# Retention of each head spread over 31 chunks of one row of main products; q, k, v and gate tiles claimed at their eviction

## The chip, the cores and the metric

The kernel runs on one core of a Trainium2 chip. The metric is device time in microseconds (us) of one execution. Three runs of the kernel before took 2264.44, 2265.14 and 2267.26 us; the median is 2265.14 us. One further execution, taken with the profiler, has a span of 2264.8 us and a time of 2266.59 us.

## The reference, cut to what matters

One layer of a decoder trunk for 256 prompt rows and 8 sample rows, so that every activation has 264 columns. The part that the change touches is the retention mixer of eight heads:

```python
h = _rmsnorm(x, norm1_g) * (1.0 + scale1) + shift1
q, k, v, gr, u, ga, gb = split(h @ w_in)
q, k = rotary(q), rotary(k) * RET_QK_DIM ** -0.5
scores = einsum('bhld,bhmd->bhlm', q, k) * decay
o = einsum('bhlm,bhmv->bhlv', scores, v) + einsum('bhld,bhdv->bhlv', q_dec, S)
S_new = gamma ** L * S + einsum('bhmd,bhmv->bhdv', k_dec, v)
y_a = (group_norm_heads(o, gn_g) * silu(gr)) @ w_proj_a
mixed = sigmoid(ga) * y_a + sigmoid(gb) * y_b
x = x + gate1 * (mixed @ w_out)
```

A head has 256 q and k columns and 512 v and gate columns. The states of the eight sample rows are read, updated and written head by head.

## The kernel before

**Products.** Every large product is made of chunks. A chunk loads 512 KB of weights (`w_...`, four blocks of 128 rows by 256 columns), splits them into a rounded part `wh_...` on ACT (line 216) and a rest `wl_...` on DVE (line 217), three buffers of each, and then issues 24 matmuls of 128x264 (line 198). A matmul triple is `wh` times the rounded activation, `wh` times its rest, and `wl` times the rounded activation, so the second matmul of a chunk already needs both parts of the activation. All these matmuls go through `mm`, which ties each to the one before it: on PE they stand in program order. Work that does not go through `mm`, as the matmuls and transposes of the retention, is placed by the scheduling layer wherever it judges it ready. The layer fixes the order of each engine's instructions when the program is built.

**The head stage.** It makes q, k, v and gate of heads 1 to 7 (`head_group`, six groups of four chunks: q, k, two of v, two of gate; head 0's come from the stage before), then the eight groups `gate_a`. Row `h` of the loop holds the groups of head h+1, and from row 1 the eight chunks `project(h-1, g)` of the previous head's output with `w_proj_a` (accumulators `acc_pa`): four after the k group, four after the first v group. Row 0 has 24 chunks, rows 1 to 6 have 32, row 7 has 32 and eight more of `gate_a`.

**Retention.** `retention(h, mods)` returns 19 steps, which `spread` deals out evenly behind the chunks of row h. The first steps are `sample_rows` (transposes `vsp`), `scores` (`scp`, then `sclo`/`schi` on DVE and ACT) and the transposes `vtp`, `ktp` of v and k with their splits `vh`, `vl`, `kh`, `kl`. Then come eight `sample(b)` (512 KB of state in and out on POOL's queue, `S` and `vb` on DVE and ACT), `prompt_out` (matmuls `op`) and `prompt_state` (`sp`), `sample_q` (`qp`) and `sample_out` (`osp`).

The last two steps are `centre` and `gate`, the group norm:

```python
mu = head_sum(o, "mu")                      # s_mu, split into s_hi_mu, s_lo_mu; two matmuls mean_mu on PE
ve.scalar_tensor_tensor(out=o, in0=mu...)   # o minus the mean, line 709
sc.activation(out=st["t4"], in_=o, func=AF.Square)
var = head_sum(st["t4"], "var")             # s_var, s_hi_var, s_lo_var; two matmuls mean_var
sc.activation(out=r, in_=var, func=AF.Sqrt, ...)
ve.reciprocal(out=r, in_=r)
ve.tensor_tensor(out=gr, in0=gr, in1=r...)  # line 724
split_act(gr, yh, yl)                       # yh on ACT, line 228; yl on DVE, line 229
```

`yh` and `yl` are what `project(h, g)` multiplies.

**Tiles.** q, k, v and gate tiles come from a pool of two buffers each. Before, the four tiles of head h+1 are claimed together at the start of row h.

Of the kernel before, what the change touches and what calls it, by code (L numbers as in the profile page):

```python
# [20 lines left out]
F32 = mybir.dt.float32  # L21
# [4 lines left out]
P = 128  # L26

D = 2048
KT = D // P
TP = 256  # L30
NS = 8
T = TP + NS
H = 8
# [11 lines left out]
G_Q, G_K, G_V, G_GR, G_U, G_GA, G_GB = 0, 8, 16, 32, 48, 56, 64  # L45
# [44 lines left out]
def spread(main, side, by=1.0):  # L90

    out, done = [], 0
    for i, step in enumerate(main):
        out.append(step)
        upto = min(int(len(side) * (i + 1) / (by * len(main))), len(side))
        out += side[done:upto]
        done = upto
    return out + side[done:]


def run(steps):
    for step in steps:
        step()


def call(f, *args):
    return lambda: f(*args)
# [22 lines left out]
def build(ctx, tc, a):  # L130
# [78 lines left out]
    def split_chunk(src, name, nk=4):  # L209
        w = raw_chunk(src, f"w_{name}", nk)  # L210
        return split_loaded(w, name, nk)
# [19 lines left out]
    def gemm_part(acc, hi, lo, xh, xl, k0, nk, first, last):  # L231

        for b in range(2):
            for k in range(nk):
                cols = slice(b * P, (b + 1) * P)
                s, e = first and k == 0, last and k == nk - 1
                mm(out=acc[:, b, :T], lhsT=hi[:, k, cols], rhs=xh[:, k0 + k, :], start=s, stop=False)
                mm(out=acc[:, b, :T], lhsT=hi[:, k, cols], rhs=xl[:, k0 + k, :], start=False, stop=False)
                mm(out=acc[:, b, :T], lhsT=lo[:, k, cols], rhs=xh[:, k0 + k, :], start=False, stop=e)

    def new_acc(name):
        n_acc[0] += 1
        return acc_ring[n_acc[0] % len(acc_ring)].tile([P, 2, 512], F32, tag="acc", name=f"acc_{name}")

    def gemm(src, gs, xh, xl, nk, name, use, apart=False):

        accs = {}
        nch = nk // 4

        def chunk(g, c):  # L250
            if c == 0:
                accs[g] = Halves([new_acc(f"{name}_{g}_{b}") for b in range(2)]) if apart else new_acc(f"{name}_{g}")
            hi, lo = split_chunk(src[g, c], f"{name}_{g}_{c}")
            gemm_part(accs[g], hi, lo, xh, xl, 4 * c, 4, c == 0, c == nch - 1)
            if c == nch - 1:
                use(g, accs[g])

        return [call(chunk, g, c) for c in range(nch) for g in gs]
# [81 lines left out]
    def rstd_from(pn, name):  # L340

        r = keep.tile([P, T], F32, tag="rstd", name=f"rstd_{name}")
        mark[name] = sc.activation(out=r, in_=pn[:, :T], func=AF.Sqrt, bias=eps[:, 0:1], scale=1.0 / D)

        for t in (slice(TP, T), slice(0, TP)) if name == "n2" else (slice(0, T),):
            ve.reciprocal(out=r[:, t], in_=r[:, t])
        return r
# [26 lines left out]
    h_hi = acts.tile([P, KT, T], F32R, tag="a_hi", name="h_hi")  # L374
    h_lo = acts.tile([P, KT, T], F32R, tag="a_lo", name="h_lo")
# [6 lines left out]
    hq = hd.enter_context(tc.tile_pool(name="qkvg", bufs=2))  # L382
    raw_q, raw_k, raw_v, raw_gr = {}, {}, {}, {}

    def head_tiles(h):
        raw_q[h] = hq.tile([P, 2, T], F32, tag="q", name=f"q{h}")
        raw_k[h] = hq.tile([P, 2, T], F32, tag="k", name=f"k{h}")
        raw_v[h] = hq.tile([P, 4, T], F32, tag="v", name=f"v{h}")
        raw_gr[h] = hq.tile([P, 4, T], F32, tag="gr", name=f"gr{h}")

    def head_groups(h):
        return [
            (G_Q + h, raw_q[h][:, 0:2]), (G_K + h, raw_k[h][:, 0:2]),
            (G_V + 2 * h, raw_v[h][:, 0:2]), (G_V + 2 * h + 1, raw_v[h][:, 2:4]),
            (G_GR + 2 * h, raw_gr[h][:, 0:2]), (G_GR + 2 * h + 1, raw_gr[h][:, 2:4]),
        ]


    with tc.tile_pool(name="pooling", bufs=1) as pl:
# [9 lines left out]
        for i in range(4):  # L409
            k = slice(4 * i, 4 * i + 4)  # L410
# [10 lines left out]
        for j in range(2):  # L421
            mark["pn"] = te.matmul(out=pn[:, :T], lhsT=ones, rhs=sgb[:, j, :], start=j == 0, stop=j == 1)
        r1 = rstd_from(pn, "n1")
        head_tiles(0)
        groups = [(G_U + g, ue[g // 2][:, 2 * (g % 2):2 * (g % 2) + 2, 15:]) for g in range(8)]
        groups += head_groups(0)
        groups += [(G_GB + g, sgb[:, 2 * g:2 * g + 2, :]) for g in range(8)]

        def start_mods(k0, nk):
# [124 lines left out]
    def rotate(x0, x1, dst, scale, name):  # L554
        cos, sin = rot[:, 0:T], rot[:, T:2 * T]
        tt = hp.tile([P, 4, T], F32, tag="t4", name=f"rot_{name}")
        for i, (s, t) in enumerate(((x0, cos), (x1, sin), (x1, cos), (x0, sin))):
            ve.scalar_tensor_tensor(out=tt[:, i, :], in0=s, scalar=scale, in1=t, op0=ALU.mult, op1=ALU.mult)
        ve.tensor_tensor(out=dst[:, 0, :], in0=tt[:, 0, :], in1=tt[:, 1, :], op=ALU.subtract)
        ve.tensor_tensor(out=dst[:, 1, :], in0=tt[:, 2, :], in1=tt[:, 3, :], op=ALU.add)  # L560

    def head_use(h, n, src):

        dst = head_groups(h)[n][1]
        if n < 2:
            rotate(src[:, 0, :], src[:, 1, :], dst, (1.0, DQK ** -0.5)[n], f"{n}_{h}")
        elif n >= 4:
            sc.activation(out=dst, in_=src, func=AF.Silu)
        elif h:
            sc.copy(out=dst, in_=src)  # L570

    def head_group(h, n):
        return gemm(a["w_in"], [head_groups(h)[n][0]], h_hi, h_lo, KT, "in",
                    lambda g, acc: head_use(h, n, acc[:, :, :T]))

    y = {}
# [173 lines left out]
    def gate_a(g):  # L750
        def use(_, acc):
            s = hp.tile([P, 2, DV], F32, tag="S", name=f"sga{g}", bufs=4)[:, :, :T]
            sc.activation(out=s, in_=acc[:, :, :T], func=AF.Sigmoid)
            sy.dma_start(out=dram["sga"][:, 2 * g:2 * g + 2, :], in_=s)

        return gemm(a["w_in"], [G_GA + g], h_hi, h_lo, KT, "ga", use)

    later = [s for i in (SC2, SH2) for s in mod2_steps(i)[1]]
    for n in range(6):
        head_use(0, n, head_groups(0)[n][1])  # L760
    for h in range(H):
        if h + 1 < H:
            head_tiles(h + 1)
            groups = [head_group(h + 1, n) for n in range(6)]
        else:
            groups = [gate_a(g) for g in range(8)]
        proj = [call(project, h - 1, g) for g in range(8)] if h else []
        mods = later[2 * h:2 * h + 2]
        main = groups[0] + groups[1] + proj[0:4] + groups[2] + proj[4:8] + groups[3] + groups[4] + groups[5]
        run(spread(main, retention(h, mods)))  # L770
        for g in groups[6:]:
            run(g)


    m_hi = acts.tile([P, KT, T], F32R, tag="a_hi", name="m_hi")
# [1 line left out]
    for g in range(8):  # L777
        k = slice(2 * g, 2 * g + 2)
# [98 lines left out]
    with tc.tile_pool(name="ffn", bufs=1) as fp:  # L877
# [19 lines left out]
        def conv_gate(i, u, cso, scv):  # L897

            c = fp.tile([P, 2, T], F32, tag="t2", name=f"cv{i}", bufs=4)
            for b in range(2):  # L900
                f = i + b * FB
                sc.activation(out=c[:, b, :], in_=u[:, b, :T], func=AF.Identity, scale=cw[:, 2, b, i:i + 1],
                              bias=vec[:, V_CB + f:V_CB + f + 1])
                for j in (1, 2):
                    ve.scalar_tensor_tensor(out=c[:, b, j:TP], in0=u[:, b, 0:TP - j], scalar=cw[:, 2 - j, b, i:i + 1],
                                            in1=c[:, b, j:TP], op0=ALU.mult, op1=ALU.add)
            ve.tensor_copy(out=cso[:, :, i % FG, 0:10], in_=u[:, :, TP - 2:T])
            ve.tensor_tensor(out=c[:, :, TP:T], in0=c[:, :, TP:T], in1=scv[:, :, i % FG, :], op=ALU.add)
            s = fp.tile([P, T], F32, tag="t1", name=f"ffs{i}", bufs=2)
            sc.activation(out=s, in_=c[:, 0, :], func=AF.Silu)  # L910
            ve.tensor_tensor(out=s, in0=s, in1=c[:, 1, :], op=ALU.mult)
            split_act(s, f_hi[:, i, :], f_lo[:, i, :])
            if i % FG == FG - 1:
                gp.dma_start(out=a["conv_out"][:, i // FG], in_=cso)

        rest = [call(gt2, 9, 1), call(gt2, 10), call(gt2, 12), call(gt2, 14)]
        for i0 in range(0, FB, FG):
            state = conv_state(i0 // FG)
            pairs = [[i0, i0 + 1]] if i0 == 0 else [[i0], [i0 + 1]]
            main = [s for gs in pairs + [[i0 + 2], [i0 + 3]]  # L920
                    for s in gemm(a["w_up"], gs, h2_hi, h2_lo, KT, "up", lambda g, acc: conv_gate(g, acc, *state))]
# [40 lines left out]
        for g in range(8):  # L962
            k = slice(2 * g, 2 * g + 2)
# [94 lines left out]
```

## Time and profile before

| | |
|---|---|
| median of 3 runs | 2265.14 us |
| profiled execution: time, span | 2266.59 us, 2264.8 us |
| PE (TensorE matmul) busy | 2236.0 us, 99% |
| PEld (TensorE weight load) busy | 2141.7 us, 95% |
| DVE (VectorE) busy | 1506.8 us, 67% |
| ACT (ScalarE) busy | 1094.3 us, 48% |
| POOL (GpSimd) busy | 222.7 us, 10% |
| head stage | about 460 to 1340 us |

A matmul's own duration is longer than the distance to the next one, since matmuls overlap; a chunk's duration is read from the chain of waits, which counts each matmul up to the start of the next. Each clock level has a share: granted clock 1.00 is 2.4 GHz, 0.50 is 1.2 GHz.

### The profile page before, as it was taken

How to read it: one execution, taken by the hardware profiler on the slowest of the kernel's cores; microseconds unless marked ns; L12 is line 12 of the kernel's file. 1: busy time of each engine (PE TensorE's matmuls, PEld its weight loads, DVE VectorE, ACT ScalarE, POOL GpSimd, SP SyncE). 2: the span in 40 equal slices, each digit the busy share in tenths (PEclk: the TensorE clock that was granted, in tenths of full speed). 3: DMA queues.
4: the chain of work that ended last, by engine and by line, in shares of the span. 5: the costliest groups of instructions: out<-in, count | busy, mean ns of one | idle time of the engine just before them, and what ended most of it. 6: DMA issues, size and time to landing. Idle time of an engine off the chain costs nothing.

```text
span 2264.8 us, 44898 instructions
## 1 busy us (share of the span) xinstructions
PE 2236.0 (99%) x18432; PEld 2141.7 (95%) x18432; DVE 1506.8 (67%) x2170; ACT 1094.3 (48%) x1380; POOL 222.7 (10%) x386
## 2 busy tenths in 40 slices
PE   8999999999999999999999999999999999999998
PEld 6899999898999999999999999899999999999998
DVE  6666775685768686868777767676666666654444
ACT  4333454354655555555556554455444444443343
POOL 0000222011101010101010101110000100000000
PEclk9999999999999999999999999999999999999999
DMA  9777867798787887878787879755656666565562
GB/s 337 245 269 260 280 195 266 283 352 311 253 297 255 290 272 270 297 258 311 249 300 252 304 264 350 261 191 183 199 186 216 209 189 211 183 191 193 184 193 100
DMA packets 168254, 561.14 MB, mean 248 GB/s; under 512 B 18448, under 2 KB 28752, under 8 KB 168048
## 3 DMA queue, kind: packets, MB, share of 16 engines
q1 hardware_dynamic: 144048, 474.08, 62.1%
q0 software_dynamic: 23568, 83.73, 10.4%
q8 instruction: 144, 2.36, 0.4%
q10 hardware_dynamic: 432, 0.46, 0.1%
q14 instruction: 62, 0.51, 0.1%
HBM read 509.82 MB, written 48.38 MB: 246 GB/s over the span
## 4 chain that ended last, share of the span: by engine, by line
PE 74%; DVE 1%; DMA 1%; issue 0%; ACT 0%; SPq 0%; DVEq 0%; ACTq 0%
PE acc_up L198 23%; PE acc_in L198 18%; PE acc_dn L198 11%; PE acc_pa L198 7%; PE acc_wo L198 4%; PE acc_ga L198 4%; PE mp L198 2%; DMA w_in<-in_w_in 1%; PE acc_dn L954 1%; PE qp L198 0%; PE scp L600 0%; DVE wl_in L217 0%; PE op L641 0%; PE op L642 0%; PE sp L651 0%
## 5 line engine op out<-in xcount | busy, mean ns | idle before, releaser
L198 PE MATMUL acc_up<-h_hi,wh_up 128*128 128x264 f32 x1408 | 400.3, 284 | 0.0
L198 PE MATMUL acc_up<-h_lo,wh_up 128*128 128x264 f32 x1408 | 399.3, 284 | 0.0
L198 PE MATMUL acc_up<-h_hi,wl_up 128*128 128x264 f32 x1408 | 399.0, 283 | 0.0
L198 PE MATMUL acc_in<-h_hi,wh_in 128*128 128x264 f32 x1344 | 385.8, 287 | 1.1 <-ACT wh_in L216 1.1
L198 PE MATMUL acc_in<-h_hi,wl_in 128*128 128x264 f32 x1344 | 382.7, 285 | 3.9 <-DVE wl_in L217 3.9
L198 PE MATMUL acc_in<-h_lo,wh_in 128*128 128x264 f32 x1344 | 383.6, 285 | 0.0
L217 DVE TENSOR_TENSOR wl_up<-w_up,wh_up 128x1024 fp32r<-128x1024 f32 x176 | 216.0, 1227 | 181.3 <-ACT wh_up L216 181.2
L216 ACT CAST wh_up<-w_up 128x1024 fp32r<-128x1024 f32 x176 | 184.6, 1049 | 251.6 <-issue 149.7
L217 DVE TENSOR_TENSOR wl_in<-w_in,wh_in 128x1024 fp32r<-128x1024 f32 x168 | 204.5, 1219 | 128.5 <-ACT wh_in L216 127.5
L216 ACT CAST wh_in<-w_in 128x1024 fp32r<-128x1024 f32 x168 | 176.0, 1049 | 193.4 <-DMA w_in<-in_w_in 92.5
L198 PEld LDWEIGHTS acc_up<-h_hi,wh_up 128*128 128x128 f32 x1408 | 264.8, 188 | 4.2 <-issue 2.5
L198 PEld LDWEIGHTS acc_up<-h_lo,wh_up 128*128 128x128 f32 x1408 | 265.0, 188 | 0.0
L198 PEld LDWEIGHTS acc_up<-h_hi,wl_up 128*128 128x128 f32 x1408 | 264.4, 188 | 0.0
L198 PEld LDWEIGHTS acc_in<-h_hi,wh_in 128*128 128x128 f32 x1344 | 254.3, 189 | 8.9 <-ACT wh_in L216 5.4
L198 PEld LDWEIGHTS acc_in<-h_hi,wl_in 128*128 128x128 f32 x1344 | 253.8, 189 | 4.9 <-DVE wl_in L217 4.8
L198 PEld LDWEIGHTS acc_in<-h_lo,wh_in 128*128 128x128 f32 x1344 | 254.3, 189 | 0.2
L198 PE MATMUL acc_st<-h_hi,wh_st 128*128 128x264 f32 x704 | 202.1, 288 | 1.0 <-ACT h_hi L363 1.0
L198 PE MATMUL acc_st<-h_hi,wl_st 128*128 128x264 f32 x704 | 200.3, 286 | 1.3 <-DVE wl_st L217 1.3
L198 PE MATMUL acc_st<-h_lo,wh_st 128*128 128x264 f32 x704 | 200.2, 285 | 0.0
L198 PE MATMUL acc_dn<-f_lo,wh_dn 128*128 128x264 f32 x680 | 192.9, 284 | 0.0
L198 PE MATMUL acc_dn<-f_hi,wl_dn 128*128 128x264 f32 x680 | 192.8, 284 | 0.0
L198 PE MATMUL acc_dn<-f_hi,wh_dn 128*128 128x264 f32 x680 | 192.8, 284 | 0.0
(273 smaller groups left out, 5357.8 us busy)
## 6 DMA issues: line engine op xcount, KB each, us to landing
wm<-in_w_mod SPq DMA_DIRECT2D x176, 512.0 KB, 6.3
w_up<-in_w_up SPq DMA_DIRECT2D x176, 512.0 KB, 4.2
w_in<-in_w_in SPq DMA_DIRECT2D x168, 512.0 KB, 5.9
w_dn<-in_w_down SPq DMA_DIRECT2D x88, 512.0 KB, 3.6
S<-in_state_ret POOLq DMA_DIRECT2D x64, 512.0 KB, 5.7
out_rs<-S POOLq DMA_DIRECT2D x64, 512.0 KB, 6.4
w_pa<-in_w_proj_a SPq DMA_DIRECT2D x64, 512.0 KB, 4.2
w_st<-in_w_in SPq DMA_DIRECT2D x66, 384.0 KB, 4.2
```

The lines of the kernel that those rows point to most:

```text
L198: ins = te.matmul(**kw)
L216: c = sc.copy(out=hi, in_=w)
L217: t = ve.tensor_tensor(out=lo, in0=w, in1=hi.bitcast(F32), op=ALU.subtract)
L954: te.matmul(out=accs[b][:, 0, t], lhsT=w[:, k, cols], rhs=f[:, kk, t], start=False, stop=e and not n, skip_group_check=n > 0)
```

## The change

The rows of the loop become one list `main` of 256 chunks, in the same order as before. Head h's retention is dealt out behind chunks 31h to 31h+30 of this list, whatever row they belong to, and the last eight chunks have no retention beside them. Head 0's 19 steps thus lie behind 31 chunks in place of 24, those of each other head behind 31 in place of 32. Where row h+1 begins at chunk 24+32h, head h's last step `gate` stands behind chunk 31h+30, and the first `project(h, 0)` is chunk 32h+32. Before, `gate` stood behind chunk 32h+23. The tiles of head h+1 are claimed one by one, each just before its first writing.

```diff
-    def head_tiles(h):
-        raw_q[h] = hq.tile([P, 2, T], F32, tag="q", name=f"q{h}")
...
+    def head_tile(h, n):
+
+        if n == 0:
+            raw_q[h] = hq.tile([P, 2, T], F32, tag="q", name=f"q{h}")
+        elif n == 1:
+            raw_k[h] = hq.tile([P, 2, T], F32, tag="k", name=f"k{h}")
+        elif n == 2:
+            raw_v[h] = hq.tile([P, 4, T], F32, tag="v", name=f"v{h}")
+        elif n == 4:
+            raw_gr[h] = hq.tile([P, 4, T], F32, tag="gr", name=f"gr{h}")
...
     def head_use(h, n, src):
 
-        dst = head_groups(h)[n][1]
+        if h:
+            head_tile(h, n)
+        dst = head_part(h, n)
...
+    main = []
     for h in range(H):
-        if h + 1 < H:
-            head_tiles(h + 1)
-            groups = [head_group(h + 1, n) for n in range(6)]
-        else:
-            groups = [gate_a(g) for g in range(8)]
+        groups = [head_group(h + 1, n) for n in range(6)] if h + 1 < H else [gate_a(g) for g in range(8)]
         proj = [call(project, h - 1, g) for g in range(8)] if h else []
-        mods = later[2 * h:2 * h + 2]
-        main = groups[0] + groups[1] + proj[0:4] + groups[2] + proj[4:8] + groups[3] + groups[4] + groups[5]
-        run(spread(main, retention(h, mods)))
-        for g in groups[6:]:
-            run(g)
+        main += groups[0] + groups[1] + proj[0:4] + groups[2] + proj[4:8] + sum(groups[3:], [])
+
+    share, steps, done = 31, [], 0
+    for i, chunk in enumerate(main):
+        chunk()
+        h = i // share
+        if i % share == 0 and h < H:
+            steps, done = retention(h, later[2 * h:2 * h + 2]), 0
+        upto = len(steps) * (i % share + 1) // share if h < H else len(steps)
+        run(steps[done:upto])
+        done = upto
```

Lines after the diff's first part move by 6 to 12; `mean_var` is line 702 before and 711 now, `op` 640 to 642 and 649 to 651.

On PE, the end of head 0's group norm and the start of its projection stand like this before. The fence has the second `mean_var` and what follows it, then the end of the stretch; between the two stand 141 matmuls of `acc_in` in all, with `vsp`, `scp`, `vtp` and `ktp` of head 1 among them.

```order
L702 MATMUL mean_var_6438<-s_lo_var_6435,ones_r 128x264
L198 MATMUL acc_in_6457<-h_hi,wh_in_2_6529 128x264
L198 MATMUL acc_in_6457<-h_lo,wh_in_2_6529 128x264
...
L198 MATMUL acc_in_6606<-h_hi,wl_in_3_6741 128x264
L198 MATMUL acc_pa_0_6775<-yh_6449,wh_pa_0_6778 128x264
L198 MATMUL acc_pa_0_6775<-yl_6450,wh_pa_0_6778 128x264
```

The same place on PE now, without a gap:

```order
L198 MATMUL acc_in_6547<-h_hi,wl_in_3_6676 128x264
L711 MATMUL mean_var_6658<-s_hi_var_6654,ones_r 128x264
L711 MATMUL mean_var_6658<-s_lo_var_6655,ones_r 128x264
L598 MATMUL vsp_6745<-cst,vsc_6743 128x128 x4
L609 MATMUL scp_6818<-q_5569,k_5751 128x256 x2
L609 MATMUL scp_6818<-q_5569,k_5751 128x128 x2
L619 MATMUL vtp_0_6860<-cst,v_5919 128x128 x4
L619 MATMUL vtp_1_6869<-cst,v_5919 128x128 x4
L198 MATMUL acc_pa_0_6711<-yh_6669,wh_pa_0_6714 128x264
L198 MATMUL acc_pa_0_6711<-yl_6670,wh_pa_0_6714 128x264
```

Of the 141 chunk matmuls between `mean_var` and the first `acc_pa` none is left; only head 1's `vsp`, `scp` and `vtp` stand there.

On DVE, head 0's group norm from its mean to `yl` reads like this now (`rot_2_6704` and `k_6703` are the rotation of the k group whose product `acc_in_6547` ends just ahead of `mean_var` on PE):

```order
L718 SCALAR_TENSOR_TENSOR o_5830<-mean_mu_6615,o_5830 128x1056
L217 TENSOR_TENSOR wl_pa_1_6756<-w_pa_1_6753,wh_pa_1_6755 128x1024
L730 SCALAR_TENSOR_TENSOR gr_158<-gr_158,vec,o_5830 128x264 x4
L704 TENSOR_TENSOR s_var_6651<-t_0_6619 128x528
L217 TENSOR_TENSOR wl_pa_2_6788<-w_pa_2_6785,wh_pa_2_6787 128x1024
L705 TENSOR_TENSOR s_var_6651<-s_var_6651 128x264
L565 SCALAR_TENSOR_TENSOR rot_2_6704<-acc_in_6547,rot 128x264 x4
L229 TENSOR_TENSOR s_lo_var_6655<-s_var_6651,s_hi_var_6654 128x264
L566 TENSOR_TENSOR k_6703<-rot_2_6704 128x264
L567 TENSOR_TENSOR k_6703<-rot_2_6704 128x264
L728 RECIPROCAL gnr_6661<-gnr_6661 128x264
L733 TENSOR_TENSOR gr_158<-gr_158,gnr_6661 128x1056
```

The next row there is `yl`. Before, the same stretch was:

```order
L695 TENSOR_TENSOR s_var_6431<-t_0_6398 128x528
L217 TENSOR_TENSOR wl_in_1_6491<-w_in_1_6488,wh_in_1_6490 128x1024
L696 TENSOR_TENSOR s_var_6431<-s_var_6431 128x264
L217 TENSOR_TENSOR wl_in_2_6530<-w_in_2_6527,wh_in_2_6529 128x1024
L229 TENSOR_TENSOR s_lo_var_6435<-s_var_6431,s_hi_var_6434 128x264
L217 TENSOR_TENSOR wl_in_3_6560<-w_in_3_6557,wh_in_3_6559 128x1024
L217 TENSOR_TENSOR wl_in_0_6610<-w_in_0_6607,wh_in_0_6609 128x1024
L719 RECIPROCAL gnr_6441<-gnr_6441 128x264
```

Before, the splits between `s_var` and the reciprocal are those of v chunks that PE multiplies meanwhile; now they are splits of the projection's own weights, and the rotation of k has moved ahead of `s_lo_var`.

On DVE at the end of head 4's group norm, from the reciprocal to `yl`, the order is now:

```order
L728 RECIPROCAL gnr_11618<-gnr_11618 128x264
L672 STREAM_SHUFFLE vb_0_11915<-vsr_11706 128x512
L611 TENSOR_TENSOR dec_11768<-scp_11770,dec_11768 128x384
L733 TENSOR_TENSOR gr_10063<-gr_10063,gnr_11618 128x1056
L565 SCALAR_TENSOR_TENSOR rot_6_11811<-acc_in_11668,rot 128x264 x4
L675 SCALAR_TENSOR_TENSOR S_0_11913<-vb_0_11915,k_10528,S_0_11913 128x512 x2
L217 TENSOR_TENSOR wl_pa_2_11927<-w_pa_2_11924,wh_pa_2_11926 128x1024
L229 TENSOR_TENSOR vl_0_11824<-vtp_0_11818,vh_0_11823 128x512
L229 TENSOR_TENSOR sclo_11777<-dec_11768,schi_11776 128x384
L229 TENSOR_TENSOR vl_1_11833<-vtp_1_11827,vh_1_11832 128x512
...
L229 TENSOR_TENSOR yl_11627<-gr_10063,yh_11626 128x1056
```

Three small rows (`k`, `kl_0`, `k`) stand where the line of dots is; `vb_0`, `S_0`, `dec`, `vl` and `sclo` belong to head 5's retention, which has moved into this stretch.

The number of chunk matmuls that PE has between the second `mean_var` of head h and its first `acc_pa` is now 0, 0, 0, 13, 23, 47, 78 and 102 for heads 0 to 7; after the first `acc_pa` matmul of heads 2, 4 and 5 stand 24 matmuls `op` of the next head's `prompt_out`, in head 3 two, ahead of the second.

## Rows read from the trace of the kernel before

**Rows 1.** The page's head and part 1: busy us, share of the span, instructions.

```profile
span 2264.8 us, 44898 instructions
PE 2236.0 (99%) x18432; PEld 2141.7 (95%) x18432; DVE 1506.8 (67%) x2170; ACT 1094.3 (48%) x1380; POOL 222.7 (10%) x386
```

**Rows 2.** Waits of PE, 420 to 640 us: total us, times, longest.

```profile
PE acc_in L198 <- DVE wl_in L217: 3.9, 4, 2.2
```

**Rows 3.** Stretches: us; busy us (instructions) by engine; granted clock; DMA share; GB/s.

```profile
467.55:470.95 3.40, 3.40 (x18) 3.40 (x18) 0.60 (x4) 1.69 (x2) 3.33 (x6) 0.50 0.99 371
543.40:556.30 12.90, 9.74 (x78) 8.44 (x69) 8.17 (x11) 6.92 (x8) 0.00 (x0) 1.00 0.76 274
556.30:559.70 3.40, 3.40 (x18) 3.40 (x17) 3.30 (x7) 1.10 (x2) 0.00 (x0) 0.50 0.77 286
```

**Rows 4.** Chain of waits, 525 to 760 us: start, us, what.

```profile
549.16 2.91 PE acc_in L198 x24
...
591.41 0.11 PE op L642
...
664.82 0.12 PE mean_mu L702
...
675.75 0.12 PE mean_var L702
...
677.84 0.44 PE vsp L589 x4
...
679.98 1.31 PE scp L600 x8
...
687.11 0.87 PE vtp L610 x8
...
694.04 2.43 PE acc_pa L198 x20
```

**Rows 5.** DVE in order of time, 664 to 700 us: start, us, instruction, idle before.

```profile
665.25 1.25 DVE L709 SCALAR_TENSOR_TENSOR o<-mean_mu,o 128x1056 f32<-128x1056 f32 x1
...
667.55 1.70 DVE L721 SCALAR_TENSOR_TENSOR gr<-gr,vec,o 128x264 f32<-128x264 f32 x4
669.16 0.70 DVE L695 TENSOR_TENSOR s_var<-t 128x528 f32<-128x528 f32 x1
...
670.92 0.43 DVE L696 TENSOR_TENSOR s_var<-s_var 128x264 f32<-128x264 f32 x1
...
672.71 0.43 DVE L229 TENSOR_TENSOR s_lo_var<-s_var,s_hi_var 128x264 fp32r<-128x264 f32 x1
...
676.42 1.80 DVE L719 RECIPROCAL gnr<-gnr 128x264 f32<-128x264 f32 x1 [0.71 <-ACT gnr L718]
678.14 1.16 DVE L217 TENSOR_TENSOR wl_in<-w_in,wh_in 128x1024 fp32r<-128x1024 f32 x1
679.22 1.24 DVE L724 TENSOR_TENSOR gr<-gr,gnr 128x1056 f32<-128x1056 f32 x1
680.38 1.44 DVE L558 SCALAR_TENSOR_TENSOR rot<-acc_in,rot 128x264 f32<-128x264 f32 x4
...
684.65 1.25 DVE L229 TENSOR_TENSOR yl<-gr,yh 128x1056 fp32r<-128x1056 f32 x1
685.82 1.41 DVE L666 SCALAR_TENSOR_TENSOR S<-vb,k,S 128x512 f32<-128x512 f32 x2
...
690.53 1.27 DVE L229 TENSOR_TENSOR vl<-vtp,vh 128x512 fp32r<-128x512 f32 x2
```

**Rows 6.** ACT in order of time, 664 to 700 us: start, us, instruction, idle before.

```profile
666.53 1.09 ACT L712 ACTIVATE t<-o 128x1056 f32<-128x1056 f32 x1 [1.05 <-DVE o L709]
...
674.47 1.28 ACT L718 ACT_TABLE_LOAD   x1
675.90 0.48 ACT L718 ACTIVATE gnr<-mean_var,eps 128x264 f32<-128x264 f32 x1 [0.15 <-PE mean_var L702]
...
681.81 1.05 ACT L228 CAST yh<-gr 128x1056 fp32r<-128x1056 f32 x1
```

## What I predict, and how

> **What bounds the kernel now.** I read the page first. PE is busy in 99% of the span and no other engine above 67%, its own weight loads apart [rows 1], so the time is PE's stream of matmuls, and a change can only shorten it by closing gaps in that stream, or lengthen it by opening some. Then I read PE's waits in the head stage: from 420 to 640 us there are four for a split on DVE, 3.9 us in all, the longest 2.2 us [rows 2]. Stretches show what such a gap costs. From 543.4 to 556.3 us, the end of head 0's retention, PE is busy 9.74 us of 12.9, so 3.2 us are open; right behind it, from 556.3 to 559.7, the granted clock is 0.50 with 18 matmuls in 3.4 us. The same fall stands at 467.55 us, before any retention runs [rows 3]. At full clock a chunk of 24 takes 2.91 us, 0.121 us each [rows 4], so 3.4 us hold 28; the second fall costs 10 to 12 matmuls, 1.2 to 1.5 us. I use 1.4.
>
> Head 0 is thus the one place with something to win: 3.2 + 1.4 = 4.6 us.
>
> **What the change does, part by part.** The number of matmuls, splits, state transfers and bytes is unchanged. Claiming a tile at its eviction adds no instruction. It could only matter where an eviction waits for the old buffer's reader, and retention h has left q, k, v and gate of head h some chunks before head h+2 writes them; I count it as nothing, and if that cover were gone it would be one chunk, 2.9 us, of waiting per head at most.
>
> *The gain.* Head 0's 19 steps get 31 chunks in place of 24. Its states and splits are less dense and the 4.6 us can go. I take the whole of it; the bounds are 0 and 4.6.
>
> *The loss.* Project(h) is not moved, but the gate that makes its input is moved to a later place, by 7 chunks for head 0 and one chunk less for every later head. What PE has between the second mean_var and the first acc_pa is what hides the end of the group norm. Before, it is 141 matmuls for head 0 (17 us) and 126 for the others: in head 1, mean_var ends at 675.87 us and acc_pa starts at 694.04, 18.2 us later, while yl is ready at 684.65 + 1.25 = 685.90 [rows 4, 5]. That is 10.0 us of work behind 18.2 us of cover. Now the cover is 0, 0, 0, 13, 23, 47, 78 and 102 matmuls, and what follows in PE's order is acc_pa.
>
> The Trainium skill, page "PSUM — Partial Sum Buffer", section "Engine vs sequencer instructions", says that matmuls start and complete in program order and that ScalarE and VectorE take their queues strictly first in, first out. By this rule no later chunk can fill the gap; without it, the gaps below would vanish. The open 3.2 us at 543.4, where PE waits with other chunks queued behind, agree.
>
> *Head 0.* I start at the end of mean_mu and add up DVE's new order. Successive rows start 0.08 us before the end of the one ahead (678.14 + 1.16 against 679.22) [rows 5], so a row counts its time less 0.08: o 1.17, a split 1.08, gr 1.62, s_var 0.62, a split 1.08, s_var 0.35, the rotation of k 1.36, s_lo 0.43, in all 7.7 us until the second mean_var. ACT's square of 1.09 us lies beside gr [rows 6]. PE has 27 matmuls left there, 3.3 us, and one mean_var of 0.1: open 4.3. From that mean_var on: 0.15 to the root on ACT, root 0.48, reciprocal 1.72, product 1.24, yh 1.05, yl 1.25, with four handovers of about 0.03: 6.0 us. The table load of 1.28 us is done while ACT waits [rows 6]. PE has mean_var 0.1, vsp 0.44, scp 1.31, vtp 0.87 and one acc_pa, together 2.9 [rows 4]: open 3.1. Head 0 loses 7.4 us.
>
> *Head 1.* The same with 41 matmuls (5.0 us) behind mean_mu and one more split ahead of s_lo: 8.8 + 6.0 − 5.0 − 0.1 − 2.9 = 6.8 us.
>
> *Heads 2 to 5.* There mean_var is in time (in head 2, 78 matmuls or 9.4 us of cover against about 9). Behind it DVE's list is again mixed with splits, rotation and the next head's first steps, so I take the 10.0 us measured in head 1 of before. Cover in PE: vsp, scp, vtp 2.6, ktp about 0.2 and one acc_pa 0.1; in heads 2, 4 and 5 the 24 op of 0.11 (2.7 us) [rows 4]; and the matmuls counted above. Head 2: 10.0 − 5.6 = 4.4. Head 3: 13 matmuls are 1.6 us, two op 0.2, so 10.0 − 4.7 = 5.3. Head 4: 23 matmuls are 2.8 us and the cover 8.4, but its list from the reciprocal to yl holds S (1.41), vl (1.27), sclo and kl (about 0.5 each) and one split fewer than in head 1: 2.3 us more, and on ACT a state of about one microsecond and the table load of 1.28 stand ahead of the root. I take 13.4 − 8.4 = 5.0. Head 5: 47 matmuls, 11.3 us of cover against 10 to 13: 1.0. Heads 6 and 7 have over 12 us of cover: nothing.
>
> The open times sum to 7.4 + 6.8 + 4.4 + 5.3 + 5.0 + 1.0 = 29.9 us.
>
> *The clock.* A gap of 3.2 us, in two parts, is followed by one fall of the clock [rows 3]. Heads 0 to 4 each have a gap at least as long, so I add one fall each, 5 × 1.4 = 7.0. The bounds are none, since a fall inside a wait costs nothing, and two falls each, 14.
>
> *Sum.* 29.9 + 7.0 − 4.6 = 32.3 us on the profiled execution's 2266.6: 2298.9. The median of the runs is 1.45 us below that execution; the forecast is 2297.5 us, slower.
>
> **Rivals.**
>
> *A, faster: the head stage only gets smoother.* The relief of head 0 decides alone, and gate is ready when acc_pa comes: 2265.1 − 4.6 = 2260.5 us. For it speaks that every gap of PE in this stage lies in head 0. It needs at most 4.6 us of new gaps, so a chain from mean_mu to yl of some 8 us in heads 0 and 1 where the rows give 13.7. Against it stand those rows. Chance 5%.
>
> *B, no change:* gaps of about 4.6 us in head 0 alone replace those that go, with the later heads covered: 2265 us. The same rows speak against it. Chance 4%.
>
> *C, a small loss: only the bare chain counts.* If DVE and ACT, with PE standing still, run ahead on everything else, the end of a group norm is 6.0 us in every head rather than 10.0. Then heads 2 and 3 lose 0.4 and 1.3, heads 4 and 5 nothing: 7.4 + 6.8 + 1.7 = 15.9 us, two falls 2.8, less 4.6: 14 us, 2279. For it: a waiting PE frees no buffer, so there is no other split to do. Against it: DVE's order is fixed, and rows queued ahead of yl are done first whatever PE does. Chance 25%.
>
> *D, a larger loss: every wait is paid twice by the clock.* Two falls in each of heads 0 to 5 (16.8 us in place of 7.0), and lists like head 4's in heads 2, 3 and 5 as well (about 2.3 us more each): 2297.5 + 9.8 + 6.9 = 2314 us. For it: two gaps of PE in this stage were each followed by a fall [rows 2, 3]. Against it: in heads 0 and 1 the wait is in two parts close together, and a fall can lie inside it. Chance 18%.
>
> The Trainium skill, page "TensorE: Matmul & The Clock Gate", section "HAM oscillation — how this bites in real kernels", describes this: waits between dense stretches of matmuls send the clock to half, and the stretch behind each starts slow. The two falls of rows 3 agree with it; how many a wait of 7 us brings no row here shows.
>
> **How the numbers follow.** The forecast holds 48%, C 25%, D 18%, A 5%, B 4%. The range goes from 2276, just below C, to 2318, just above D, which leaves out A, B and the outer ends of C and D. About 0.2% (4.5 us) is what a measurement of this kernel can tell from no change. Faster by more than that: 5%, rival A, whose 4.6 us barely pass that mark. Within it: 5%. Slower: 90%.
>
> **What the profile after would show.** In PE's waits there should be entries that were absent: acc_pa for yh on ACT and yl on DVE, and mean_var for s_lo_var, each a few us in heads 0 and 1, acc_pa alone in heads 2 to 4, little in head 5, none in heads 6 and 7. The granted clock should fall near each of them, and the gap at 543 us should be gone or smaller. PE's matmul count stays. From 1340 us of before on, everything should look the same, shifted. I am wrong if acc_pa follows vtp directly in heads 0 and 1; if heads 2 to 4 wait 2 us or less, it is C; if the clock stays at 0.50 for more than 3.4 us per head, D.

## The result and the profile after

The changed kernel takes 2318.52 us (median of 4 runs, 2314.75 to 2325.87) against 2264.79 us (2264.39 to 2267.26). The ratio is 1.023 with a 95% interval of [1.0215, 1.0245]: slower, as forecast, but by 53.7 us and not by 32.3. The forecast's range ended at 2318 us, so the time lies on its upper edge: half a microsecond above it by this median, just inside it (2317.2 us) when the ratio is applied to the median of 2265.14 us that the forecast started from. The profiled execution of the changed kernel is the fastest of its four, 2314.75 us.

The page's head and part 1 of the changed kernel, which answer to [rows 1]:

```profile
span 2313.0 us, 44919 instructions
PE 2255.5 (98%) x18432; PEld 2155.7 (93%) x18432; DVE 1509.6 (65%) x2170; ACT 1097.2 (47%) x1381; POOL 225.3 (10%) x386
```

The matmuls are as many as before. PE is busy 19.5 us longer with the same work, which is what a slower clock looks like in this line (the mean granted clock is 0.988, and was 0.997), and the rest of the 48.2 us by which the span grew is waiting. The share of PE moved by one point; it would be easy to read past it.

All of it lies in the head stage. From the first acc_in (465.0 us) to the first acc_wo (1367.4 us) before takes 902.4 us and after 952.1, 49.7 more. The waits of PE from 560 to 1400 us in the changed kernel (us in total, times, longest):

```profile
PE op L649 <- DVE vl L229: 6.7, 4, 2.8
PE mean_var L711 <- ACT s_hi_var L228: 5.3, 2, 3.6
PE ktp L629 <- DVE dec L611: 5.2, 3, 2.6
PE osp L698 <- ACT qs L693: 3.6, 2, 3.4
PE mean_var L711 <- DVE s_lo_var L229: 2.6, 2, 2.0
PE acc_pa L198 <- ACT yh L228: 2.5, 2, 2.0
PE acc_pa L198 <- DVE yl L229: 2.3, 3, 0.9
```

None of these seven stands in [rows 2]. A crossing is here the place on PE where the end of a head's group norm, from mean_mu to yl, meets the first products of its projection; its cover is the number of chunk matmuls between the second mean_var and the first acc_pa. mean_var and acc_pa are the forecast's; op and ktp are the same crossings caught one step earlier; osp is something else. Head 0's crossing on PE (start, us, instruction, idle before it):

```profile
573.14 0.28 PE L198 MATMUL acc_in<-h_hi,wl_in 128*128 128x264 f32 x1
577.03 0.59 PE L711 MATMUL mean_var<-s_hi_var,ones_r 128*128 128x264 f32 x1 [3.61 <-ACT s_hi_var L228]
578.24 0.59 PE L711 MATMUL mean_var<-s_lo_var,ones_r 128*128 128x264 f32 x1 [0.61 <-DVE s_lo_var L229]
579.40 1.12 PE L598 MATMUL vsp<-cst,vsc 128*128 128x128 f32 x4 [0.58 <-POOL vsc L595]
580.31 2.77 PE L609 MATMUL scp<-q,k 128*128 128x256 f32 x8
...
584.92 0.39 PE L198 MATMUL acc_pa<-yl,wh_pa 128*128 128x264 f32 x1 [0.83 <-DVE yl L229]
```

And on DVE in the same microseconds, answering to [rows 5]:

```profile
570.17 1.26 DVE L718 SCALAR_TENSOR_TENSOR o<-mean_mu,o 128x1056 f32<-128x1056 f32 x1 [0.55 <-PE mean_mu L711]
...
577.76 0.42 DVE L229 TENSOR_TENSOR s_lo_var<-s_var,s_hi_var 128x264 fp32r<-128x264 f32 x1
...
579.37 1.80 DVE L728 RECIPROCAL gnr<-gnr 128x264 f32<-128x264 f32 x1 [0.51 <-ACT gnr L727]
581.21 1.26 DVE L733 TENSOR_TENSOR gr<-gr,gnr 128x1056 f32<-128x1056 f32 x1
583.61 1.26 DVE L229 TENSOR_TENSOR yl<-gr,yh 128x1056 fp32r<-128x1056 f32 x1 [1.14 <-ACT yh L228]
```

From o at 570.17 to the end of s_lo_var at 578.18 are 8.0 us (forecast 7.7), from there to the end of yl at 584.87 are 6.7 (forecast 6.0). From the start of scp to that of the next matmul are 2.56 us here, where its eight matmuls took 1.31 in [rows 4]: it runs at half clock. The clock fell at 576.2, inside the wait that began at 573.4, and stayed down until 583.0; yl is ready only at 584.87, so scp at half clock ran under the chain on DVE, and PE still waited for it. These are all the stretches of the stage at 0.50 (us; busy us by PE, PEld, DVE, ACT, POOL; granted clock; DMA share; GB/s), against the two of [rows 3]:

```profile
576.20:583.00 6.80, 4.77 (x15) 3.82 (x16) 5.73 (x10) 3.26 (x5) 1.00 (x1) 0.50 0.27 77
695.60:699.00 3.40, 2.91 (x10) 2.55 (x11) 3.06 (x2) 0.83 (x2) 0.44 (x1) 0.50 0.40 146
815.10:821.90 6.80, 6.77 (x33) 6.59 (x32) 2.20 (x4) 1.54 (x3) 0.00 (x0) 0.50 0.11 31
931.10:941.30 10.20, 7.91 (x30) 6.75 (x31) 7.61 (x15) 2.94 (x5) 0.71 (x1) 0.50 0.38 122
1050.60:1060.80 10.20, 7.85 (x35) 7.67 (x36) 6.76 (x11) 2.27 (x4) 1.43 (x2) 0.50 0.54 174
1139.40:1142.80 3.40, 3.40 (x18) 3.40 (x16) 2.78 (x5) 0.58 (x1) 0.00 (x0) 0.50 1.01 411
1173.50:1180.30 6.80, 6.80 (x34) 6.80 (x33) 6.14 (x13) 1.44 (x3) 0.72 (x1) 0.50 0.51 176
```

Together PE is busy 40.4 us in them and does what takes half of that at full clock: by this estimate about 20 us of matmul time are added, where before two falls added 3. Not all of it is lost, since in heads 0 and 1 the fall lies wholly inside the wait.

To separate waiting from clock I counted every interval between the starts of neighbouring matmuls that is longer than usual for that pair: inside a stretch at 0.50 up to a doubling is clock, all else is waiting. An undisturbed 32 chunks of before hold 5.3 us of small intervals of this kind; they are taken off. Which of the two an interval goes to is a convention: time at half clock that passes under a wait is counted as clock here.

| | forecast, us | counted, us |
|---|---|---|
| waits at head 0, 1 | 7.4, 6.8 | 6.1, 6.2 |
| heads 2, 3, 4 | 4.4, 5.3, 5.0 | 6.9, 6.0, 7.8 |
| head 5 | 1.0 | 4.1, and 3.7 at osp |
| heads 6, 7 | 0 | 0.5, 0 |
| clock | 7.0 | 18.1 |
| gain | −4.6 | −9.0 |
| sum | 32.3 | 50.4 |

The stage itself grew by 49.7. The gain is 2.6 us of waiting in the gap at 543 us, 3.3 us of shorter intervals and both falls of before, 3.1. The shorter intervals don't lie at the very start of the stage: its first eight chunks take 29.0 us before and 27.5 after, and those 1.5 us are the fall at 467.55.

### The profile page after: what moved, and what is told of

The parts are those of the page before. It is cut to its first block, busy times and chain, and to the rows that moved or that the text cites. A ratio compares the mean times of both kernels' runs of the same rounds, so it can differ in the third digit from the quotient of the medians.

```text
span 2313.0 us, 44919 instructions
## 1 busy us (share of the span) xinstructions
PE 2255.5 (98%) x18432; PEld 2155.7 (93%) x18432; DVE 1509.6 (65%) x2170; ACT 1097.2 (47%) x1381; POOL 225.3 (10%) x386
```

## The experiments

Ratios are to the kernel before, run beside each on the same chip. The first four ask which part of the change costs; "main" is the list of chunks that PE works through, "proj" the eight chunks of project(h), "groups" the six of the next head.

**The claims alone.** The kernel before with tiles claimed at their eviction, nothing else:

```
-    def head_tiles(h): ...          # q, k, v, gate of the next head, all at once
+    def head_tile(h, n): ...        # one of them, from its eviction
```

> The kernel before with only the claims changed: q, k, v and gate tiles claimed one by one at their eviction, the spread as it was. The instructions stand in the same order on PE as in the kernel before. Theory: the claims cost and bring nothing, 2263 to 2268 us. Rival (claims at the eviction make evictions wait for the old buffer): some us slower, 2270 us or more.

2266.76 us (10 runs), ratio 0.9991 [0.9981, 1.0002]. PE, DVE and ACT execute the same instructions in the same order as before. The claims cost nothing; what is left for the loss is the spreading. For the gain it is less clear: in the profiled execution of this run the head stage takes 898.5 us, 3.9 less than before, and though PE still waits 2.2 us for a split near the end of head 0's retention, no fall of the clock follows there. Whether that is the claims' doing or chance of one execution, the ratio can't tell.

**The projection early, without the change.** The kernel before, with project(h) ahead of the group norm's end, so that no chunk covers it:

```
-        main = groups[0] + groups[1] + proj[0:4] + groups[2] + proj[4:8] + groups[3] + groups[4] + groups[5]
+        main = groups[0][:1] + proj[0:4] + groups[0][1:] + groups[1] + proj[4:8] + sum(groups[2:6], [])
```

> The kernel before, spread over 24 or 32 chunks of one row as it was, but with project(h, 0 to 3) put behind the first chunk of the next row and project(h, 4 to 7) behind its k group. Cover behind mean_var is then 0 matmuls for heads 0 to 6 where it was 126 to 141. Theory (cover): seven crossings of some 6 us of waiting and 2.5 us of clock each, 60 us, 2310 to 2340 us. Rival (the spread over 31 is what costs): no change, 2263 to 2268 us.

2326.03 us (4 runs), ratio 1.0248 [1.0234, 1.0262]. A loss as large as that of the change is produced without the change. PE's largest waits in its head stage:

```profile
PE mean_var L702 <- ACT s_hi_var L228: 8.6, 6, 1.6
PE acc_in L198 <- DVE wl_in L217: 6.7, 6, 2.2
PE mean_var L702 <- DVE s_lo_var L229: 5.5, 7, 0.9
PE acc_pa L198 <- DVE yl L229: 5.0, 7, 0.9
PE acc_pa L198 <- ACT yh L228: 4.5, 2, 3.0
```

Here retention is not yet in the next chunk of work, so ktp and op don't appear, and the chain shows in the forecast's own places: mean_var, yl and yh count 23.6 us. Not all of this loss is the chain's: the splits wl_in, of which the kernel before has 3.9 us, count 6.7, and y_a, the sum that the projection's accumulators are added to, another 8.2.

**The projection late, with the change.** One line of the changed kernel:

```
-        main += groups[0] + groups[1] + proj[0:4] + groups[2] + proj[4:8] + sum(groups[3:], [])
+        main += sum(groups[0:4], []) + proj[0:4] + groups[4] + proj[4:8] + sum(groups[5:], [])
```

> The kernel after, with project(h, 0 to 3) put behind the second v group and project(h, 4 to 7) behind the first gate group of the next row, eight chunks later than now. Spread, claims, work and bytes as in the kernel after; PE then has 116, 134, 174, 188, 215, 239, 270 and 102 chunk matmuls between the second mean_var and the first acc_pa of heads 0 to 7. Theory (cover: the loss is PE waiting for the group norm because too few chunks stand ahead of acc_pa): all 35 us of waits and 15 us of clock go, head 0's relief stays, 2258 to 2266 us. Rival (the loss comes from the 31-chunk spread itself, its denser steps and transfers): stays at 2310 to 2320 us. Second rival (half of it is the table of steps, not the cover): about 2290 us.

2287.02 us (6 runs), ratio 1.0078 [1.0064, 1.0093]. The expected 2258 to 2266 us was missed. Two thirds of the loss go, and with them every wait of mean_var, yl, ktp and op. What remains is new: PE's acc_pa waits 11.8 us in five places for an eviction of gate on ACT and 4.5 in two places for y_a and a sample state there, and ACT's copy of a state waits 28.6 us for the store of the one before it (4.4 in the changed kernel).

**Waits filled.** The changed kernel, with 24 matmuls for each of heads 0 to 5 at the start of project, 144 in all (17.4 us at 0.121), whose result nobody reads:

```
+        if g == 0 and h < 6:
+            for i in range(24):
+                mm(out=acc[:, 0, :T], lhsT=ones_r, rhs=h_hi[:, i % KT, :], start=True, stop=True)
```

> The kernel after with 24 more matmuls of 128x264 per head for heads 0 to 5, ahead of project(h, 0), written into its accumulator and overwritten by its first product: 144 matmuls that nobody reads, 17.4 us of PE work at full clock. Theory (a third of the loss is the clock falling after waits): they run inside waits of 6 to 8 us per head and keep PE active, so the falls get fewer and the time drops below 2318.5 us, to 2300 to 2313 us, though more is computed. Rival (the falls overlap the waits and cost little, and the filling delays mean_var or acc_pa): slower, up to 2336 us. Third: no change, 2316 to 2321 us.

2310.77 us (4 runs), ratio 1.0183 [1.0165, 1.0201], below the 1.0215 at which the changed kernel's interval begins: more work, less time. (The changed kernel was not run again beside it.) Its stretches at half clock:

```profile
581.50:584.90 3.40, 3.00 (x10) 2.64 (x11) 3.06 (x2) 0.82 (x3) 0.35 (x1) 0.50 0.08 25
704.40:707.80 3.40, 3.40 (x16) 3.40 (x17) 1.88 (x4) 0.29 (x1) 0.00 (x0) 0.50 0.19 58
820.40:823.80 3.40, 3.40 (x19) 3.40 (x18) 0.71 (x1) 0.59 (x1) 0.00 (x0) 0.51 0.20 58
1049.10:1059.30 10.20, 8.63 (x40) 8.63 (x41) 5.43 (x10) 1.77 (x4) 1.33 (x2) 0.50 0.56 174
```

20.4 us in place of 47.6. The head stage takes 941.4 us, 10.7 less than in the changed kernel; 27.2 us less at half clock are worth up to 13.6 by the estimate above. The filling took the place of waiting and cannot shorten the chain that PE waits for, and DVE's order is the same but for 15 of 2170 instructions; so what it gave back is read as clock. The clock is then a cost of its own, at least in part.

**How much cover is enough.** Four runs move the projection, the end of retention, or both. In the changed kernel the steps of a head end after a fixed 31 chunks; in these they end at a given chunk, two or four later than in the kernel before:

```
-    share, steps, done = 31, [], 0
+    ends = [24 + 32 * h + 2 for h in range(H)]      # + 4 in the second
```

The projection moves from behind groups 1 and 2 to behind groups 2 and 3 (four chunks). First that alone:

> The kernel after with project(h, 0 to 3) put behind the first v group and project(h, 4 to 7) behind the second, four chunks later than now, so that no projection follows a gate group as in the first late version. The 31-chunk spread stays. Cover behind mean_var is 20, 38, 78, 109, 119, 143, 174 and 126 matmuls. Theory (cover): head 0 waits about 5 us, head 1 about 2.5, the others nothing, one or two falls of the clock, less the relief of head 0 (4.9 us): 2264 to 2274 us, or a ratio to the kernel before of 0.999 to 1.003. Rival (the spread over 31 itself costs, as the 0.8% of the first late version could mean): ratio 1.007 or more.

2287.36 us (4 runs), ratio 1.0088 [1.0072, 1.0105]. The expected 0.999 to 1.003 was missed. Heads 0 and 1, with 20 and 38 matmuls of cover, wait 4.5 and 2.6 us. But PE also waits 3.5 us at 964, for the eviction v on ACT, and 2.0 us at 1087, for y_a on DVE, each followed by a fall of the clock. ACT ahead of the first:

```profile
965.39 0.58 ACT L663 COPY so<-sp 128x512 f32<-128x512 f32 x1 [7.02 <-DMA out_rp<-so]
965.87 1.05 ACT L216 CAST wh_pa<-w_pa 128x1024 fp32r<-128x1024 f32 x1
966.82 0.60 ACT L579 COPY v<-acc_in 128x528 f32<-128x528 f32 x1
```

The state copy so has one buffer, shared with the copy qs ahead of osp, and stands 7.02 us at the head of ACT's queue until the store of the one before has landed; the weight cast and the eviction v that PE wants stand behind it. The rival, that the spread over 31 costs by itself, is not excluded by this run.

Then the end of retention two chunks later than in the kernel before, with the projection where it always was:

> Each head's retention ends two chunks later than in the kernel before (head 0 over 26 chunks, the others over 32, 30 chunks in the last), projections where they were. Cover behind mean_var is 78 matmuls in every head. Theory (cover): 9.4 us and vsp, scp, vtp hide the 10 us, nothing waits; head 0 is relieved by part of its 4.9 us: ratio 0.998 to 1.0. Rival (any shift of the retention against the rows costs in proportion): two sevenths of 2.3%, ratio about 1.006.

2264.2 us (12 runs), ratio 0.998 [0.9969, 0.9992]. As expected: every crossing has 78 matmuls of cover and no wait of one is left. Two chunks further:

> The same with four chunks later (head 0 over 28). Cover is 0 in head 0, 13 in heads 1 to 5, 30 in heads 6 and 7. Theory (cover): it falls off a cliff: eight crossings of 4 to 7 us of waiting and 2 us of clock each, 45 to 60 us less 4 of relief, ratio 1.018 to 1.025, as much as the kernel after though the shift is smaller for head 0. Rival (in proportion to the shift): ratio about 1.012.

2325.09 us (4 runs), ratio 1.0246 [1.023, 1.0263]. Two chunks more in each head and the whole loss is back, at all eight crossings, with 13 matmuls of cover in most heads. PE's waits there:

```profile
PE ktp L629 <- DVE dec L611: 13.1, 5, 2.6
PE acc_pa L198 <- ACT yh L228: 6.0, 4, 3.9
PE op L649 <- DVE vl L229: 5.9, 6, 1.8
PE acc_pa L198 <- DVE yl L229: 4.3, 7, 0.7
```

And both moved by four, so that the distance between them is that of the kernel before again:

> Both together: retention ends four chunks later than in the kernel before (head 0 over 28 chunks, the last head over 28) and the projections stand behind the two v groups, four chunks later too. Cover is 91 in head 0, 102 to 126 in the others. Theory (cover): no waits at the crossings, and head 0's relief is left: 4.9 us below the kernel before at best, ratio 0.9975 to 0.9995. Rival (the relief only moves the gap to another place, as the kernel after has a new one at 1135 us behind late weights): ratio 1.0 to 1.002.

2267.73 us (11 runs), ratio 0.9996 [0.9987, 1.0005]: no change, and between the two expectations. No crossing waits. One gap of 2.5 us is left at 1286 us, for y_a. For the waits at the crossings it is the distance between the last step of a head and its projection that decides, not the place of either.

**A version that beats both.** Both shifts were made to shrink towards the last heads, so that the last head is not squeezed, once from four with the projection four later, once from two:

```
+    ends = [24 + 32 * h + min(4, 7 - h) for h in range(H)]      # first
+    ends = [24 + 32 * h + min(2, 7 - h) for h in range(H)]      # second
```

> Both shifts by four chunks, tapered at the end: head h's retention ends 4, 4, 4, 4, 3, 2, 1, 0 chunks later than in the kernel before, so that the last heads keep 31 chunks each; projections behind the two v groups. Cover behind mean_var is 91, 109, 109, 109, 119, 143, 174 and 126 matmuls. The combination with four everywhere had one gap left, 2.65 us at 1285 us, where the last head's 28 chunks made weights late, and one fall of the clock. Theory (cover and relief, the gap at 1285 is the denser last head): that gap goes, ratio 0.996 to 0.999. Rival (projections behind v groups cost by themselves, as the waits at 963 and 1087 us of the 31-chunk version with the same place): ratio 1.001 or more.

2271.87 us (12 runs), ratio 1.0017 [1.0003, 1.0031]: here the rival's number came and not the expected 0.996 to 0.999. There is one wait of 4.3 us at 952, again an acc_pa for the eviction v, again with the state copy held (7.81 us). Heads 4 to 7, which have 31 chunks each here, show no wait at their crossings.

> Two chunks later, tapered (2 for heads 0 to 5, then 1 and 0), projections where they were. Cover is 78 matmuls for heads 0 to 6 and 102 for head 7. Theory: the same as with two everywhere, ratio 0.997 to 0.9995, since its stretch shows no waits at any crossing. Rival (that run's 0.998 was the luck of the runs): ratio 1.0.

2264.2 us (7 runs), ratio 0.9971 [0.9961, 0.9982]: 0.3% or some 6.6 us faster than the kernel before, and 2.5% faster than the changed one. From 480 to 1420 us PE has three waits left, of 0.6, 0.5 and 0.4 us, and its head stage holds no stretch at 0.50. Against the claims alone (0.9991, an interval that just touches this one) the spread's own part of this gain is not settled.

**The held copy.** The last two runs let ACT issue the store of the state itself, where it stood in GpSimd's queue behind the sample states; once with the projection four chunks later, once in the changed kernel:

```
-            gp.dma_start(out=a["rp"][h, d * P:(d + 1) * P, :], in_=so)
+            sc.dma_start(out=a["rp"][h, d * P:(d + 1) * P, :], in_=so)
```

> The kernel of the run with the projection behind groups 2 and 3 (ratio 1.0088 to the kernel before), with one edit: the DMA that stores a head's new state, out_rp, is issued by ScalarE right behind the copy that fills its tile, and no longer by GpSimd, whose queue holds it back behind the sample states. Nothing else moves. My theory of the rest of that run's loss: the copy so has one buffer, the next one waits until the store of the one before has landed (22.4 us of waits by ScalarE, 7.0 us the longest), the weight casts stand behind it on ScalarE, and TensorE waits at 963 us (3.68 us) and 1087 us (2.16 us) and pays with the half clock. Expected then: the waits of so for out_rp under 6 us in all, no gap of TensorE over 1.5 us outside the crossings of heads 0 and 1, and a ratio of 1.0035 to 1.006, since heads 0 and 1 keep their 5 and 2.1 us of waits and their clock. Rival: the gaps come from the v groups' own load on VectorE and ScalarE, or from the state loads on the DMA rings; then they stay about where they are and the ratio stays at 1.0075 to 1.0095.

2282.24 us (6 runs), ratio 1.0059 [1.0047, 1.0071], below 1.0088 by a third and with intervals that just don't overlap. The gaps at 964 and 1087 us are gone, and the clock falls only behind heads 0 and 1. One part missed: the copy still waits 16.1 us for its store, not under 6:

```profile
ACT so L663 <- DMA out_rp<-so: 16.1, 6, 4.0
```

The longest is 4.0 us in place of 7.0, short enough for PE not to notice. So the place in GpSimd's queue was a part of the wait; what makes up the rest was not taken apart.

> The changed kernel with the same single edit: out_rp is issued by ScalarE and no longer by GpSimd. In the changed kernel the copy so waited for out_rp once, 4.4 us, and no gap of TensorE that I attribute to the crossings stands behind it. My theory (the loss is the crossings' chain and the half clock that follows): the ratio stays at that of the changed kernel, 1.021 to 1.024. Rival: the held copy is behind a part of the crossings' waits too (ScalarE late with s_hi_var, yh and qs); then the ratio falls below 1.020.

2312.93 us (5 runs), ratio 1.0204 [1.0187, 1.0222], between the two expectations, with an interval that overlaps that of the changed kernel. All the crossings still wait. The wait of osp at 1135 us is absent, but osp also stands a few matmuls later in PE's order here, so this does not tell what caused it.

## Why the prediction was right, and where it was short

The direction and the mechanism came as forecast; the size did not. By the counts above, heads 2 to 5, osp, head 6 and the clock were put 24.4 us too low, the waits of heads 0 and 1 were put 1.9 too high and the gain 4.4 too small, which leaves 18.1. That the time still touches the range is in part luck: two of the errors took from the others.

**The mechanism is the forecast's.** The gate's steps were moved towards a projection that stays; the group norm's chain came out uncovered on PE, where chunks that stood further back in its order did not fill the 3.61 us at 573. The run with the early projection makes as large a loss without the change, and the runs with shifts of two and four turn it off and on. Claims at no cost, heads 6 and 7 at nothing, the matmul count and the gone gap at 543 us hold as well.

**Heads 0 and 1** were right in size: 6.1 and 6.2 us of waiting, and half of the 4.77 and 2.91 us that PE was busy at half clock there (3.8 us, an estimate), make 16.1 us, where waits of 7.4 and 6.8 and two falls of 1.4 make 17.0. The split is another one. The chain in head 0 took 14.7 us and not 13.7, and the clock cost little of its own, since the matmuls at half clock ran while yl was still being made. In head 1 it is the same: the clock is back at 699.0, and yl starts after that.

```profile
700.11 1.26 DVE L229 TENSOR_TENSOR yl<-gr,yh 128x1056 fp32r<-128x1056 f32 x1 [1.14 <-ACT yh L228]
```

So one named sign of being wrong does appear in head 0: the first acc_pa follows vtp directly, at 583.72. The wait stands one matmul later, for yl.

**Heads 2 to 5: the cover was counted too long.** The step that took ktp and the op matmuls as cover in PE failed. They are retention of the next head, and they wait on DVE too: for dec, which frees the buffer ktp writes, and for vl. DVE has these in the same queue as the group norm. In head 4, DVE and then PE:

```profile
1044.43 1.80 DVE L728 RECIPROCAL gnr<-gnr 128x264 f32<-128x264 f32 x1 [1.52 <-ACT gnr L727]
1046.16 0.72 DVE L672 STREAM_SHUFFLE vb<-vsr 128x512 f32<-128x512 f32 x1
1046.78 0.54 DVE L611 TENSOR_TENSOR dec<-scp,dec 128x384 f32<-128x384 f32 x1
1047.23 1.25 DVE L733 TENSOR_TENSOR gr<-gr,gnr 128x1056 f32<-128x1056 f32 x1
1048.40 1.44 DVE L565 SCALAR_TENSOR_TENSOR rot<-acc_in,rot 128x264 f32<-128x264 f32 x4
1049.76 1.40 DVE L675 SCALAR_TENSOR_TENSOR S<-vb,k,S 128x512 f32<-128x512 f32 x2
1051.08 1.22 DVE L217 TENSOR_TENSOR wl_pa<-w_pa,wh_pa 128x1024 fp32r<-128x1024 f32 x1
1052.22 0.68 DVE L229 TENSOR_TENSOR vl<-vtp,vh 128x512 fp32r<-128x512 f32 x1
```

```profile
1047.37 0.44 PE L629 MATMUL ktp<-cst,k 128*128 128x128 f32 x2 [1.07 <-DVE dec L611]
1049.79 0.39 PE L198 MATMUL acc_pa<-yh,wh_pa 128*128 128x264 f32 x1 [1.98 <-ACT yh L228]
1052.95 0.58 PE L649 MATMUL op<-schi,vh 128*128 128x256 f32 x1 [2.77 <-DVE vl L229]
```

dec stands behind a reciprocal that is itself waiting, and vl behind gr, rot, a state and a weight split. Three short waits follow each other, and the op that should have covered the chain waits longest. Heads 2 to 5 counted 24.8 us, osp left out, where 15.7 were forecast: 9.1 us. In heads 2, 4 and 5, the three whose sums took 24 op as 2.7 us of cover, the miss is 2.5, 2.8 and 3.1; in head 3, with two op, it is 0.7. (For head 4 the terms that the forecast names add up to 14.6 us and not to the 13.4 that it took; that alone would have made its 5.0 into 6.2.)

**The clock was mis-sized most.** I took one fall of 1.4 us for each of five heads, 7.0; it counted 18.1, 11.1 more. About 4 of the 18.1 lie inside the waits of heads 0 and 1; some 14 are left behind the others. One fall of 3.4 us [rows 3] was carried over to every crossing. The clock stayed at 0.50 for 6.8 us in heads 0, 2 and 5, for 10.2 in heads 3 and 4, and for 3.4 in head 1 and behind osp. What makes one crossing hold it down longer than another is not shown. It is not only that the waits come in pieces: with the projection four later, a single wait of 3.5 us was followed by 6.8 us at 0.50, and with the claims alone a wait of 2.2 us by no fall at all.

By the forecast's own sign, a clock that stays at 0.50 for more than 3.4 us per head, this is rival D, whose 2314 us also lie nearer to the time than the forecast's 2297.5. D's clock term (16.8 us) was close. Its other term, 2.3 us more in heads 2, 3 and 5 for lists like head 4's, fits the misses of heads 2 and 5 but not those of heads 3 (0.7) and 4 (2.8), which the lost cover of the op fits.

**Osp** (3.7 us and a fall) was in no list. PE waits there for a copy on ACT that stands behind three weight casts, which wait 5.48, 2.24 and 3.53 us for their weights, with the DMA share at 1.01 just after. Of the three profiled kernels with this spread and this place of the projection, the changed kernel and its filled version (2.0 us) have this wait, and the one with the store moved has not. What makes the difference was not shown.

**The gain** was put too low: 9.0 us where 4.6 was taken. The gap at 543 us went as forecast, 2.6 us of 3.2, with the fall behind it. Not in the sum were the fall at 467.55, gone too, and 3.3 us of shorter intervals in the first row. How much of it the spread brings and how much the claims or chance is open, as the run with the claims alone shows.

**What the late projection leaves.** With the store moved as well, the head stage is 9.0 us longer than in the kernel before (911.4 against 902.4). By the count above heads 0 and 1 have 10.3 us of waiting and 4.8 of clock there; less a gain of 9.0 that is 6.1, and the other 2.9 were not placed. The ratio of 1.0059 is 13.4 us, 4.4 more than the stage. Outside the head stage the two profiled executions differ by 4.9 us (1367.3 against 1362.4), but there the profiled executions of all these kernels scatter from 1360.9 to 1368.8 us.

## What to carry to other kernels

When steps are spread over a stream of matmuls, measure the distance from the last step to the first matmul that needs its result, in matmuls, against the chain between them: here 78 were enough and 13 in most heads cost 2.5%. In the changed kernel, with the shift of four and with the projection four later, PE's waits at one crossing summed to 4.5 us with 20 matmuls, 5.8 with 23, 2.4 and 4.6 with 30, 2.6 with 38 and 2.3 with 47, against 4.0 to 4.2 with 13. Count as cover only matmuls that do not wait on the engine that runs the chain. Price a crossing by all its waits, and the clock behind them as a range: here it stayed at 0.50 for nothing to 10.2 us.

## What was unexpected

144 matmuls that compute nothing made the kernel 0.47 points faster, because stretches at 0.50 fell from 47.6 to 20.4 us.

Between a shift of two chunks and one of four, 5.8 us of PE's work at full clock, lies a step from 0.998 to 1.0246. The expectation by cover had forecast it. What it had not is that the waits do not simply grow as the cover shrinks: 23 matmuls left 5.8 us of waiting and 13 left 4.2. That the splits, rotations and states of the next head stand in other places in DVE's queue each time may be the reason; no run shows it.

A copy of 0.58 us held ACT's queue for 7.02 us, because its only buffer was still being stored; the changed kernel had one such wait, of 4.4 us, and whether it had a part in the loss stayed open (ratio 1.0204 with the store moved, intervals that overlap).
